# The up-projection's and the last stage's split operands in many memory forms

## The chip, the cores and the metric

The kernel runs on one core of a Trainium2 chip. The metric is the device time in microseconds (us) of one execution, as the median of several runs; lower is better. The engines are named as in the profile: PE is the matrix engine's multiplication, PEld its load of the stationary operand, DVE the vector engine, ACT the scalar engine, POOL the general one, SP the engine that issues most DMAs.

## The reference

One decoder layer on 256 tokens of width 2048: a mixer (mLSTM and RWKV-7 in parallel), cross-attention into 256 memory tokens, and a convolutional gated feed-forward part. All values are float32. The part that the change touches is the last:

```python
def conv_glu_ffn(h, w_up, conv_w, conv_b, w_down):
    u = h @ w_up                                   # (256, 2048) @ (2048, 16384)
    uc = conv_b + sum(conv_w[j] * shift_right(u, CONV_WIDTH - 1 - j) for j in range(CONV_WIDTH))
    gate, up = split_cols(uc, (D_FF, D_FF))
    return (jax.nn.gelu(gate, approximate=True) * up) @ w_down   # (256, 8192) @ (8192, 2048)
...
    h = rms_norm(x, ffn_pre_norm[l])
    x = x + rms_norm(conv_glu_ffn(h, ffn_w_up[l], ffn_conv_w[l], ffn_conv_b[l], ffn_w_down[l]), ffn_post_norm[l])
```

## The kernel before

**Split operands.** PE multiplies in the type float32r, which keeps fewer bits than float32. So each large operand is split in two: `hi` is the value rounded to float32r (ACT writes it) and `lo` is the value minus `hi` (DVE writes it). A product of weights and activations is then three matmuls into the same accumulator: weight `hi` by activation `hi`, weight `hi` by activation `lo`, weight `lo` by activation `hi`. Each matmul first loads a stationary operand of 128 columns (PEld) and then streams a moving operand past it (PE).

**The feed of weights.** All weights come as items of 128 x 1024 float32 (512 KB) by DMA into tiles `raw` (four buffers). `Feed.hi` has ACT cast an item to `wh` (L391), `Feed.lo` has DVE subtract to get `wl` (L421); `wh` and `wl` are tiles of 1152 elements per partition with four buffers each, of which `staged` hands out a view that begins at element 0 or 16. The engines' orders are written out by hand in `run()`: before the matmuls of item i it emits the staging of items up to i + 3, so the staged weights lie some items ahead of PE. The table `KICK` gives 19 items of the earlier stages another view: it begins at element 24 in place of 16, or its second half lies 8 or 24 elements further, so that one or both halves of the item begin 8 elements (32 bytes) off a multiple of 16 elements (64 bytes). Item 18, for instance, has both halves off.

**The up-projection** (tiles `fm`) is 32 blocks of 512 columns. A block is 8 items; an item holds two chunks k of 128 input features. Per chunk and 128 columns the weights are stationary (128 columns of `wh` or `wl`) and the activations `fh`, `fl` (128 x 256 tokens of chunk k) are moving: 2 x 4 x 3 = 24 matmuls an item, 192 a block, 6144 in all. The `hT` tiles `fh` and `fl` hold 16 chunks of 256 elements each and lie apart. After a block DVE and ACT work out the convolution and the gate and leave the result in `ac`. Blocks 0 and 1 are interleaved with each other.

**The last stage** (tiles `tm`) is the down-projection: 2 blocks of 1024 columns, 64 items each, one chunk k per item. Here the activations are stationary: `asplit` splits two chunks of `ac` at a time into a tile `as` (`hi` of both, then `lo` of both), and the weights move, 512 columns at a time: 4 accumulators x 3 = 12 matmuls an item, 1536 in all. The last 4 items of the second block are taken accumulator by accumulator. The norm and the output follow.

`mm` (L181) issues every matmul, `Meter.call` (L66) records most operations of ACT and DVE, so many rows of the profile bear those two lines. The tile `hT` has two buffers; they hold in turn `hh`/`hl`, `mh`/`ml`, `fh`/`fl`, and at the end `gain` and one `z3`.

Of the kernel before, what the change touches and what calls it, by code (L numbers as in the profile page):

```python
# [145 lines left out]
def _layer(ctx, tc, nc, d, dbg):  # L146
# [18 lines left out]
    def hT(name):  # L165
        return mp.tile([P, KD, S], F32R, tag="hT", bufs=2, name=name)
# [12 lines left out]

    def mm(out, lhsT, rhs, start=True, stop=True):  # L180
        pe.matmul(out, lhsT, rhs, start=start, stop=stop, skip_group_check=True)  # L181
# [163 lines left out]
    class Feed:  # L345
        def __init__(self, order):
# [27 lines left out]
        def staged(self, name, r, i):  # L374


            k, c = r.shape[1:]
            kick = KICK.get(i)
# [4 lines left out]
            w = wp.tile([P, 1024 + 128], F32R, tag=name, bufs=4, name=name)  # L383
            return w[:, o:o + k * e].rearrange("p (k c) -> p k c", k=k)[:, :, 0:c]

        def hi(self, upto):
            while self.ns <= min(upto, len(self.src) - 1):
                self.dma(self.ns)
                r = self.raw[self.ns]
                wh = self.staged("wh", r, self.ns)  # L390
                nc.scalar.copy(wh, r)  # L391
                self.st[self.ns] = [wh, None]
                self.ns += 1
# [22 lines left out]
        def lo(self, upto):  # L416
            self.hi(upto)
            while self.nl <= min(upto, len(self.src) - 1):
                r = self.raw.pop(self.nl)
                wl = self.staged("wl", r, self.nl)  # L420
                nc.vector.tensor_sub(wl, r, self.st[self.nl][0])  # L421
                self.st[self.nl][1] = wl
                self.nl += 1
# [10 lines left out]
    def tm_products(o, t, c, wx, first, last):  # L434
        wh, wl, xh, xl = wx
        t = slice(t // P * P, t // P * P + P)
        c = slice(c, c + o.shape[1])
        mm(o, xh[:, t], wh[:, c], start=first, stop=False)
        mm(o, xl[:, t], wh[:, c], start=False, stop=False)
        mm(o, xh[:, t], wl[:, c], start=False, stop=last)  # L440
# [16 lines left out]
    def run():  # L457
        order = visits()
        feed = Feed([("xv" if b is xv else b["kind"], s) for b, c0, c1 in order for s in b["srcs"][c0:c1]])
# [6 lines left out]
        for b, c0, c1 in order:  # L466
# [23 lines left out]
            for ci, s in enumerate(srcs):  # L490
# [13 lines left out]
                for kj in range(s.shape[1]):  # L504
                    xh, xl = b["xs"](k) if kj else ahead
                    first, last = k == 0, k == nk - 1
                    if b["kind"] == "fm":
                        steps = []
                        for m in range(nm):
                            o = banks[m // 2][:, m % 2]  # L510
                            a, c = wh[:, kj, m * P:(m + 1) * P], wl[:, kj, m * P:(m + 1) * P]
                            steps.append([(o, a, xh, first and m % 2 == 0, False), (o, c, xh, False, last),
                                          (o, a, xl, False, False)])
# [14 lines left out]
                    elif b is xv:  # L528
                        for g in range(2):
                            halves(banks, (wh[:, kj], wl[:, kj], xh, xl), first, last, g)  # L530
                    else:
                        for g, o in enumerate(banks):
                            n = o.shape[1]
                            tm_products(o, g * P * n // b["cols"], g * n % b["cols"], (wh[:, kj], wl[:, kj], xh, xl),
                                        first, last)
                            if len(banks) == 4 and g == 1:
                                side.half()
# [59 lines left out]
    hh, hl = hT("hh"), hT("hl")  # L597
# [903 lines left out]
    class Residual:  # L1501
# [8 lines left out]
        def run(self):  # L1510
# [12 lines left out]
            def parts(i, js=(0, 1)):  # L1523
                for j in js:
                    k = i * 2 + j
                    act.activation(hi[:, k], part(xr, i)[:, j], AF.Identity, scale=pcol(gname, k))
                for j in js:
                    k = i * 2 + j
                    dve.scalar_tensor_tensor(lo[:, k], part(xr, i)[:, j], pcol(gname, k), hi[:, k],
# [99 lines left out]
    def mem_prep():  # L1629
        M["mh"], M["ml"] = hT("mh"), hT("ml")  # L1630
# [177 lines left out]
    def start_ffn():  # L1808
# [3 lines left out]
        M["res"] = Residual(st3, "z2", stf, hT("fh"), hT("fl"), "fg", False)  # L1812
# [58 lines left out]
    for b in range(32):  # L1871
        fu = block("fm", W("w_fu", b), fu_xs(b), fu_evac(b),
              before=start_ffn if b == 0 else None, pool_=aux if b == 2 else acc)
        if b < 2:
# [4 lines left out]
    def asplit(k):  # L1879

        if k not in M["as"]:
            n = k // 2
            if k == 126:
                a = C("as", "bg0", [P, 1024], F32R)
            else:
                a = mp.tile([P, 1024 + 128], F32R, tag=f"au{n % 2}", bufs=1, name="as")[:, 0:1024]
            a = a.rearrange("p (i j s) -> p i j s", i=2, j=2)
            a, b_ = a[:, 0], a[:, 1]
            for j in range(2):
                split(a[:, j], b_[:, j], actile((k + j) % 64))  # L1890
# [33 lines left out]
    def load_gain():  # L1924
        M["gain"] = mp.tile([P, D], F32, tag="hT", bufs=2, name="gain")
# [4 lines left out]
    def fd_evac(n):  # L1930

        def gen(ps):
            if n:
                z = mp.tile([P, 2, 1024], F32, tag="hT", bufs=2, name="z3")
# [70 lines left out]
    for n in range(2):  # L2005
        block("tm", W("w_fd", n), ax(n), fd_evac(n), cols=1024, pool_=acc if n else aux,
              tail=4 if n else 0)
# [93 lines left out]
```

## Time and profile before

| | |
|---|---|
| median of 2 runs | 1865.76 us (1865.25 and 1866.28) |
| span of the profiled execution | 1863.2 us; the runs' median lies 2.6 us above it |
| granted PE clock | 0.999 |
| PE busy | 1853.5 us (99%) |
| PEld busy | 1767.5 us (95%) |
| DVE busy | 1295.5 us (70%) |
| ACT busy | 1017.0 us (55%) |
| up-projection, last stage | about 807 to 1507 us, and 1507 to 1856 us of the span |

A row of instructions names the line, the engine, the operation, the tiles as output<-inputs, the shape, and then busy time and the mean of one in ns. PE's matmuls are pipelined: the duration of one (277 ns for 256 columns) is longer than the distance from its start to the next one's start, and that distance is what a stream of them costs. It is read from the chain of waits (time by number of matmuls) or from the starts in the timeline.

### The profile page before, as it was taken

What the parts mean: (1) busy time and instruction counts of PE and PEld (TensorE: products, weight loads), DVE (VectorE), ACT (ScalarE), POOL (GpSimd) and SP (SyncE); (2) the same over time, 40 slices, a digit from 0 to 9 for tenths busy, and PEclk for the clock granted to TensorE, in tenths of its full rate; (3) what the DMA queues carried; (4) which work ended last, traced back from release to release, by engine and by line L of the source; (5) the groups of instructions that cost most, each with busy time, mean ns of one, the idle gap of its engine ahead of it and who ended that gap; (6) DMA issues with size and microseconds to landing.
All of it is one profiled execution on the core that took longest, in us unless ns stands there. A gap on an engine that the chain in (4) does not pass through costs nothing.

```text
span 1863.2 us, 36212 instructions
## 1 busy us (share of the span) xinstructions
PE 1853.5 (99%) x14934; PEld 1767.5 (95%) x14934; DVE 1295.5 (70%) x1832; ACT 1017.0 (55%) x1492; POOL 32.4 (2%) x62
## 2 busy tenths in 40 slices
PE   9999999999999999999999999999999999999998
PEld 9999988999999999999999999999999988888887
DVE  7789777566675857787766667776666775556555
ACT  6876445655454646665554455444445554545544
POOL 0000020000000000000000000000000000000000
PEclk9999999999999999999999999999999999999999
DMA  7556544344555765555666666666666666666664
GB/s 261 186 166 203 180 149 160 136 160 158 172 195 196 277 197 180 165 180 172 202 192 194 196 195 196 185 194 199 195 194 195 197 192 215 194 193 192 194 192 145
DMA packets 98198, 351.47 MB, mean 189 GB/s; under 512 B 11056, under 2 KB 11568, under 8 KB 97648
## 3 DMA queue, kind: packets, MB, share of 16 engines
q1 hardware_dynamic: 97168, 348.01, 58.6%
q8 instruction: 117, 1.92, 0.4%
q10 hardware_dynamic: 864, 1.15, 0.2%
q14 instruction: 49, 0.40, 0.1%
HBM read 347.01 MB, written 2.10 MB: 187 GB/s over the span
## 4 chain that ended last, share of the span: by engine, by line
PE 98%; DVE 1%; DMA 0%; issue 0%; ACT 0%; ACTq 0%; DVEq 0%
PE fm L181 68%; PE tm L181 25%; PE gram L181 0%; DVE wl L421 0%; PE Y L181 0%; DMA w<-in_w_in_dram 0%; PE num L181 0%; PE lv L181 0%; DVE ql L66 0%; PE X L181 0%; PE U L181 0%; PE zg L181 0%; DVE z L66 0%; PE zwa L181 0%; PE xsc L181 0%
## 5 line engine op out<-in xcount | busy, mean ns | idle before, releaser
L421 DVE TENSOR_TENSOR wl<-raw,wh 128x1024 fp32r<-128x1024 f32 (+1 forms) x639 | 774.8, 1218 | 412.7 <-ACT wh L391 406.5
L391 ACT CAST wh<-raw 128x1024 fp32r<-128x1024 f32 (+1 forms) x639 | 663.6, 1043 | 476.0 <-PE fm L181 362.5
L181 PE MATMUL fm<-fh,wh 128*128 128x256 f32 x2048 | 564.2, 277 | 0.6 <-DVE fh L66 0.6
L181 PE MATMUL fm<-fh,wl 128*128 128x256 f32 x2048 | 563.2, 276 | 0.0
L181 PE MATMUL fm<-fl,wh 128*128 128x256 f32 x2048 | 563.2, 276 | 0.0
L181 PEld LDWEIGHTS fm<-fh,wh 128*128 128x128 f32 x2048 | 383.6, 188 | 0.8 <-DVE fh L66 0.8
L181 PEld LDWEIGHTS fm<-fl,wh 128*128 128x128 f32 x2048 | 383.5, 188 | 0.0
L181 PEld LDWEIGHTS fm<-fh,wl 128*128 128x128 f32 x2048 | 383.5, 188 | 0.0
L181 PE MATMUL tm<-wh,as 128*128 128x512 f32 x1024 | 315.1, 389 | 0.0
L181 PE MATMUL fm<-hh,wh 128*128 128x256 f32 x1024 | 284.3, 280 | 1.7 <-ACT wh L402 1.5
L181 PE MATMUL fm<-hl,wh 128*128 128x256 f32 x1024 | 281.7, 277 | 0.0
L181 PE MATMUL fm<-hh,wl 128*128 128x256 f32 x1024 | 281.5, 277 | 0.1
L181 PEld LDWEIGHTS tm<-wh,as 128*128 128x128 f32 x1024 | 192.2, 188 | 39.8
L181 PE MATMUL tm<-wl,as 128*128 128x512 f32 x512 | 199.2, 389 | 0.0
L181 PEld LDWEIGHTS fm<-hh,wh 128*128 128x128 f32 x1024 | 191.9, 188 | 3.4 <-ACT wh L402 1.7
L181 PEld LDWEIGHTS fm<-hl,wh 128*128 128x128 f32 x1024 | 191.9, 188 | 0.1
L181 PEld LDWEIGHTS fm<-hh,wl 128*128 128x128 f32 x1024 | 191.5, 188 | 0.3 <-DVE wl L421 0.3
L181 PEld LDWEIGHTS tm<-wl,as 128*128 128x128 f32 x512 | 96.1, 188 | 19.9
L66 ACT CAST as<-ac 128x256 fp32r<-128x256 f32 x128 | 45.6, 404 | 110.8 <-PE tm L181 110.8
L66 DVE TENSOR_TENSOR as<-ac,as 128x256 fp32r<-128x256 f32 x128 | 48.6, 421 | 61.7 <-ACT as L66 61.7
L181 PE MATMUL fm<-mgh,wh 128*128 128x256 f32 x256 | 70.9, 277 | 0.0
L181 PE MATMUL fm<-mgl,wh 128*128 128x256 f32 x256 | 70.8, 276 | 0.0
(406 smaller groups left out, 2225.0 us busy)
## 6 DMA issues: line engine op xcount, KB each, us to landing
raw<-in_w_fu_dram SPq DMA_DIRECT2D x256, 512.0 KB, 4.1
raw<-in_w_in_dram SPq DMA_DIRECT2D x152, 512.0 KB, 3.6
raw<-in_w_fd_dram SPq DMA_DIRECT2D x128, 512.0 KB, 3.9
raw<-in_w_br_dram SPq DMA_DIRECT2D x32, 512.0 KB, 4.1
raw<-in_w_mo_dram SPq DMA_DIRECT2D x32, 512.0 KB, 4.3
raw<-in_w_xk_dram SPq DMA_DIRECT2D x8, 512.0 KB, 4.2
raw<-in_w_xv_dram SPq DMA_DIRECT2D x8, 512.0 KB, 3.6
raw<-in_w_xq_dram SPq DMA_DIRECT2D x8, 512.0 KB, 4.0
```

The costliest lines, as they stand in the source:

```text
L66: return f(out, *a, **k)
L181: pe.matmul(out, lhsT, rhs, start=start, stop=stop, skip_group_check=True)
L391: nc.scalar.copy(wh, r)
L421: nc.vector.tensor_sub(wl, r, self.st[self.nl][0])
```

## The change

The `hi` and `lo` of one operand now share one tile, and where in it they lie follows tables. All numbers in the tables are elements of 4 bytes. `halves_of(v, g)` cuts a view in two: with g = 0 the first and the second half, with g = 1 the even and the odd elements, with a larger g alternating groups of g elements.

- `STATIONARY`, one entry per up-projection block from block 2 on: the weights' form. (0, a, b) is `hi` beginning at element a and `lo` at element 1152 + b of a `w2` tile of 2304. (1, a) is `hi` and `lo` element by element in turn from element a on. Blocks 2, 12, 13, 30 and 31 have both at multiples of 16; blocks 3 to 11 have both off a multiple of 16; blocks 14, 16, 19, 21 have only `lo` off and 15, 17, 18, 20 only `hi`; blocks 22 to 29 are element by element.
- `MOVING`, one entry per pair of chunks of the up-projection (so one per item of each block): the activations' form, (g, offset). Items 0 and 1 of a block are two halves at offsets 0 and 16, item 2 at offset 8, items 3, 4, 5, 6, 7 alternate in groups of 1, 4, 8, 32 and 2.
- `STREAMED`, per pair of items of the last stage, eight entries in rotation: the moving weights at offsets 0, 16, 8, 24, then alternating in groups of 16 and of 4, then two entries with plain halves but another width: 512 columns are taken as 256 + 256, or as 384 + 128. The last four items of the second block keep the plain form and 512.
- `HELD`, per 16 chunks of the last stage over both blocks: the stationary activations at offsets 0, 16, 8, 24, then element by element, then offset 4, element by element from 16, and 0.

What is computed is the same, and the output accumulators have the same shapes. The tile `hT` becomes one tile of 16 x 528 elements with one buffer; the earlier users of it get two halves of it that lie as before.

```diff
-    def hT(name):
-        return mp.tile([P, KD, S], F32R, tag="hT", bufs=2, name=name)
+    def hT(name, dt=F32R):
+        return mp.tile([P, KD * 528], dt, tag="hT", bufs=1, name=name)
+    MOVING = [(0, 0), (0, 16), (0, 8), (1, 0), (4, 0), (8, 0), (32, 0), (2, 0)]
+    STATIONARY = [(0, 16, 16), (0, 16, 16), (0, 0, 0), (0, 2, 2), (0, 4, 4), (0, 6, 6), (0, 8, 8), (0, 12, 12),
+                  (0, 20, 20), (0, 24, 24), (0, 28, 28), (0, 30, 30), (0, 16, 0), (0, 0, 16), (0, 16, 24), (0, 24, 16),
+                  (0, 16, 8), (0, 8, 16), (0, 20, 16), (0, 16, 20), (0, 12, 16), (0, 16, 12), (1, 0), (1, 4), (1, 8),
+                  (1, 12), (1, 16), (1, 20), (1, 24), (1, 28), (0, 16, 16), (0, 16, 16)]
+    STREAMED = [(0, 0, 512), (0, 16, 512), (0, 8, 512), (0, 24, 512), (16, 0, 512), (4, 0, 512), (0, 0, 256), (0, 0, 384)]
+    HELD = [(0, 0), (0, 16), (0, 8), (0, 24), (1, 0), (0, 4), (1, 16), (0, 0)]
+    class Halves:
+        def __init__(self, v, i):
+            v = v.rearrange("p (k c) -> p k c", k=KD)
+            self.v = [halves_of(v[:, k, o:o + 512], g)[i] for k in range(KD) for g, o in (MOVING[k // 2],)]
...
+    def halves_of(v, g):
+        n = v.shape[1] // 2
+        if g == 0:
+            return v[:, 0:n], v[:, n:2 * n]
+        if g == 1:
+            v = v.rearrange("p (l i) -> p i l", i=2)
+        else:
+            v = v.rearrange("p (l i g) -> p i l g", i=2, g=g)
+        return v[:, 0], v[:, 1]
...
+            lo = name == "wl"
+            if not lo:
+                self.pairs[i] = wp.tile([P, 2304], F32R, tag="w2", bufs=4, name="w2")
+            w = self.pairs[i]
+            form = self.form.get(i)
+            if form:
+                g, o = form[0], form[1]
+                if g:
+                    return halves_of(w[:, o:o + 2048], g)[lo].rearrange(
+                        "p (k l) -> p k l" if g == 1 else "p (k l) g -> p k l g", k=k)
+                o = 1152 + form[2] if lo else o
+                return w[:, o:o + 1024].rearrange("p (k c) -> p k c", k=k)
...
-    def tm_products(o, t, c, wx, first, last):
+    def tm_products(o, t, c, wx, first, last, width=512):
...
+        for a in range(0, n, width):
+            b = min(a + width, n)
+            q, hi, lo = o[:, a:b], part_of(wh, c + a, c + b), part_of(wl, c + a, c + b)
+            mm(q, xh, hi, start=first and a == 0, stop=False)
+            mm(q, xl, hi, start=False, stop=False)
+            mm(q, xh, lo, start=False, stop=last)
...
+            if b.get("ups", 0) > 1:
+                form[at] = STATIONARY[b["ups"]]
+            if "down" in b and (b["down"], j) < (1, 60):
+                g, o, n = STREAMED[j // 2 % 8]
+                form[at] = (g, o, o)
...
+            g, o = HELD[k // 16]
...
-                a = mp.tile([P, 1024 + 128], F32R, tag=f"au{n % 2}", bufs=1, name="as")[:, 0:1024]
-            a = a.rearrange("p (i j s) -> p i j s", i=2, j=2)
-            a, b_ = a[:, 0], a[:, 1]
+                a = mp.tile([P, 1024 + 128], F32R, tag=f"au{n % 2}", bufs=1, name="as")[:, o:o + 1024]
+            a, b_ = [v.rearrange("p (j s) g -> p j s g" if g > 1 else "p (j s) -> p j s", j=2) for v in halves_of(a, g)]
```

Two places of the engines' orders show what moves. The first is PE's order in the last stage, at chunk 14 of the first block, ahead and now (`tm_n` are the four accumulators, `as` the stationary activations, the last numbers the output's shape). Before:

```order
L181 MATMUL tm_18531<-wh_18782,as_18800 128x512 x2
L181 MATMUL tm_18531<-wl_18784,as_18800 128x512
L181 MATMUL tm_18532<-wh_18782,as_18800 128x512 x2
L181 MATMUL tm_18532<-wl_18784,as_18800 128x512
L181 MATMUL tm_18533<-wh_18782,as_18800 128x512 x2
L181 MATMUL tm_18533<-wl_18784,as_18800 128x512
L181 MATMUL tm_18534<-wh_18782,as_18800 128x512 x2
L181 MATMUL tm_18534<-wl_18784,as_18800 128x512
```

And now:

```order
L230 MATMUL tm_18005<-w2_18245,as_18262 128x384 x3
L230 MATMUL tm_18005<-w2_18245,as_18262 128x128 x3
L230 MATMUL tm_18006<-w2_18245,as_18262 128x384 x3
L230 MATMUL tm_18006<-w2_18245,as_18262 128x128 x3
L230 MATMUL tm_18007<-w2_18245,as_18262 128x384 x3
L230 MATMUL tm_18007<-w2_18245,as_18262 128x128 x3
L230 MATMUL tm_18008<-w2_18245,as_18262 128x384 x3
L230 MATMUL tm_18008<-w2_18245,as_18262 128x128 x3
```

Twelve matmuls of 512 columns have become twelve of 384 and twelve of 128, each with its own load of a stationary operand. Where the width is 256, there are 24 of 256 in their place. Over both blocks 28 items are so cut, 14 with 256 and 14 with 384, and PE has 336 matmuls more.

The second is DVE's order in the up-projection, with the semaphores that a row waits for (`us`, `tg`, `tu`, `ac` belong to the convolution and the gate of the block before). Before:

```order
L66 SCALAR_TENSOR_TENSOR tu_15599<-us_15595,cv_9869,tu_15599 128x254 [waits DVE_49]
L421 TENSOR_TENSOR wl_15678<-raw_15566,wh_15676 128x1024 [waits DMAHW7_49,PE_49,Activation_49]
L66 TENSOR_TENSOR ac_15694<-tg_15596,tu_15598 128x256
L66 TENSOR_TENSOR ac_15694<-tg_15597,tu_15599 128x256 [waits DVE_49]
L421 TENSOR_TENSOR wl_15711<-raw_15605,wh_15709 128x1024 [waits DMAHW0_49,PE_49,Activation_49]
```

And now:

```order
L66 SCALAR_TENSOR_TENSOR tu_15161<-us_15157,cv_9601,tu_15161 128x254 [waits DVE_49]
L484 TENSOR_TENSOR w2_15236<-raw_15128,w2_15236 128x1024 [waits DMAHW7_49,Activation_49]
L66 TENSOR_TENSOR ac_15253<-tg_15158,tu_15160 128x256
L66 TENSOR_TENSOR ac_15253<-tg_15159,tu_15161 128x256 [waits DVE_49]
L484 TENSOR_TENSOR w2_15268<-raw_15166,w2_15268 128x1024 [waits DMAHW0_49,Activation_49]
```

The order of the operations on DVE and on ACT is the same. DVE's subtraction no longer waits for PE, since the buffer is now taken when ACT writes `hi`; ACT's cast waits for the last reader of both halves.

More of the change, by code (lines that the diff above doesn't have):

```diff
@@ L345, in _layer, with __init__ @@
     class Feed:
-        def __init__(self, order):
+        def __init__(self, order, form):
+            self.form, self.pairs = form, {}
             self.kind = [k for k, s in order]
```

66 lines of the change are left out of this document (46 added, 20 removed).

## The prediction

> **What bounds the kernel now.** I read the clock and the span first, then the engines' shares and the chain of waits, then the chain in order of time, then the stretches of the two stages that change.
>
> ```profile
> core 0: 1863.2 us, clock 0.999
> PE 1853.5 (99%) x14934; PEld 1767.5 (95%) x14934; DVE 1295.5 (70%) x1832; ACT 1017.0 (55%) x1492; POOL 32.4 (2%) x62
> PE 98%; DVE 1%; DMA 0%; issue 0%; ACT 0%; ACTq 0%; DVEq 0%
> 938.94 568.50 PE fm L181 x5016
> 1507.44 348.20 PE tm L181 x1536
> 939.00:1507.00 568.00, 392.87 (x526) 1.00 0.64 194
> ```
>
> The clock is full, and the chain is PE for 98%. In the two stages it is nothing else: 568.50 / 5016 = 113.3 ns from one matmul of 256 columns to the next, 348.20 / 1536 = 226.7 ns for 512, which is exactly twice as much. So the price goes by the streamed column (0.443 ns), and no fixed price per matmul or per load shows. The last row is DVE alone in the up-projection: 392.87 of 568 us, 69%. PE has no idle time to give or to hide in: whatever makes a matmul start later lengthens the kernel one for one.
>
> How near is the load of the stationary operand to becoming the limit? The four loads ahead of matmuls with one moving column show it, since there nothing else takes time:
>
> ```profile
> 755.16 0.52 PEld L181 LDWEIGHTS st<-ones,stx 128*128 128x128 f32 x4 [0.26 <-DVE stx L66]
> L181 PEld LDWEIGHTS fm<-fh,wh 128*128 128x128 f32 x2048 | 383.6, 188 | 0.8 <-DVE fh L66 0.8
> ```
>
> Four loads of 188 ns each fill 520 ns, so they start (520 - 188) / 3 = 111 ns apart. With 113.3 ns per matmul the up-projection has only 2 ns to spare; with 226.7 the last stage has 115. That bounds any gain: if a form took moving columns faster, the loads would hold the 6144 matmuls at 111 ns, 14 us less, 0.8%.
>
> **The change part by part.** First the narrower width. Of 28 cut items 14 go as 256 + 256, 2 x 113.3 = 226.7 ns, nothing lost. The other 14 x 12 = 168 matmuls become 384 (170.0 ns at 0.443 a column) and 128. By the column 128 would cost 56.7 and the whole nothing; but each has a load, and those keep 111 ns. 170.0 + 111 - 226.7 = 54 ns, times 168: **+9 us**, between 0 and 9. I take 9, since three of 128 follow each other and leave a load nothing to hide behind.
>
> Second, stationary weights off the 64-byte grid. The items of KICK in the kernel before show that. These starts are of item 18, both halves 32 bytes off, and of a later one:
>
> ```profile
> 50.93 0.28 PE L181 MATMUL fm<-hh,wh 128*128 128x256 f32 x1
> ...
> 53.09 0.28 PE L181 MATMUL fm<-hh,wh 128*128 128x256 f32 x1
> 717.96 0.28 PE L181 MATMUL fm<-mh,wh 128*128 128x256 f32 x1
> ...
> 719.13 0.28 PE L181 MATMUL fm<-ml,wh 128*128 128x256 f32 x1
> ```
>
> Between the first two lie 18 steps, 120 ns each; between the others 10, 117 ns each. So off the grid costs 4 to 7 ns a matmul, with no other change. Blocks 3 to 11 are off for all 9 x 192 = 1728 matmuls; of the eight blocks with one half off, `hi` is stationary twice and `lo` once in three, so half of 1536 are off: 768. Third, the 8 x 192 = 1536 loads element by element: no row shows one. Their ends are 0 (the load keeps its 111 ns) and twice a load, 222 ns, that is +109 each. I take 4.7, as for the off-grid loads, the nearest row with a load from an unusual place. Together 2496 + 1536 = 4032 matmuls at 4.7 ns; one in eight runs under item 3, below, where the moving side hides it: 3528 x 4.7 = **+17 us**, between 0 (if the other offsets and the steps are free) and 25 at 7 ns; with doubled loads 1344 x 109 = 146 more.
>
> Fourth, the moving activations. All moving operands of the trace are contiguous and on the grid, so the price has to be argued from how much slack the stream has. Two rows speak:
>
> ```profile
> 859.13 0.44 PE xt L1920 x4
> L1920 PE MATMUL xt<-con,xr x32: 270/273/273, 859.0 to 938.7; 128*128 128x128 f32 x32
> ```
>
> The transposes stream 128 columns of 4 bytes in 0.44 / 4 = 110 ns, 0.86 ns a column. That is half the rate, and a little less than twice 0.443 = 0.886: the fast stream pays some 3% that the slow one does not, as a stream would that is just short of data. If so, a read that fetches two neighbours and throws one away halves the rate: item 3 (element by element) has 32 x 24 = 768 matmuls, and each would take 226.7 in place of 113.3, **+87 us**. Its ends are 0 and 87, and I take 87. The groups of 2 (item 7) use whole pairs; if the unit fetched is 16 bytes, they halve too, +87 more. I leave them at the small price and keep the 87 for the range. Items 2, 4, 5 and 7 in the seven blocks with loads on the grid: 7 x 4 x 24 = 672 matmuls at between 0 and 7 ns, 3.5 taken: **+2 us**. Item 6 (groups of 32, runs of 128 bytes) costs 0.
>
> By the Trainium skill's page "TensorE: Matmul & The Clock Gate", section "Part 1: The HAM clock gate", a warm stream takes 1 / 2.4 GHz = 0.417 ns a column and 2.5 ns a matmul, 109 ns here by an estimate; the trace's 113.3 is above that, and its surcharge goes by the column.
>
> Fifth, the last stage. Loads have 115 ns to spare, so off-grid or stepped stationary activations (80 of the 128 chunks) hide behind the moving weights up to a doubled load. The moving weights are off the grid in a quarter of the items and grouped by 16 or 4 in another: 768 matmuls at 0 to 14 ns (7 per 256 columns), 4 taken: **+3 us**.
>
> Sixth, DVE and ACT. They write `hi` and `lo` with a step of two elements in blocks 22 to 29 and read `hi` so. Rows on what steps cost DVE:
>
> ```profile
> L421 DVE TENSOR_TENSOR wl<-raw,wh 128x1024 fp32r<-128x1024 f32 x631 | 768.7, 1223 | 409.7 <-ACT wh L391 403.5 <-PE fm L181 4.7
> L66 DVE TENSOR_TENSOR ac<-tg,tu 128x256 f32<-128x256 f32 x64 | 24.1, 419 | 0.0
> L66 DVE TENSOR_TENSOR mt<-cmt,con 128x256 f32<-128x256 f32 x8 | 4.6, 619 | 0.0
> L391 ACT CAST wh<-raw 128x1024 fp32r<-128x1024 f32 x631 | 658.1, 1048 | 470.4 <-PE fm L181 360.5 <-PE tm L181 89.9 <-ACT wh L391 4.8
> 939.00:1507.00 568.00, 255.80 (x209) 1.00 0.64 194
> ```
>
> `cmt` is read with a step of 32 elements: 200 ns more for 256, 0.78 ns an element. The last row is `wl` alone: 255.8 of DVE's 392.9 us, so the rest is 137 us in 568, 5.3 in a block's 21.8. With eight subtractions of 1.22 that is 15.0 us, and PE's 21.8 covers it. One stepped operand makes 2.0 us of each (21.4 in all, still covered), two make 2.8 (27.9: not covered). But item 3 then takes 24 x 113 ns = 2.7 us longer too, so PE's block is 24.5 or more. Taken: 0; at worst 27.9 - 24.5 = 3.4 a block, 27 us in eight. ACT's cast is 1048 ns; doubled it is 16.8 us a block beside about 4 of its own, covered.
>
> The queues: no instruction is moved past another on ACT, DVE, POOL or SP. ACT's cast now waits for the last reader of `lo` as well, one matmul (113 ns) later than for `hi`; its idle time in the row above, mostly for PE, is 470 us, and DVE's subtraction, which follows it, has three items' lead. Cost 0; if the lead were gone, 256 items x 0.1 us, 26 us.
>
> The sum: 1863.2 + 9 + 17 + 87 + 2 + 3 = 1981 us of span, and 2.6 us more for the median of the runs, which lies that far above the span: **1984 us**, +6%.
>
> **The rivals.** *Steps are free for the moving side, places cost a little.* Without the 87 us, but with item 3's 768 matmuls now at up to 7 ns and its loads not hidden, +3: 1984 - 87 + 3 = **1900 us**, +1.8%. For it: 0.443 ns is the same for 256 and for 512 columns, so it may be the stream's own pace and no shortage of data. Against it: the 0.86 of the half-rate stream.
> A rule of the Trainium skill gives this case: "SBUF — State Buffer", section "Door 1: The DMA port swizzle", says that memory lines are 16 bytes and that two hits per line give full bandwidth. Every second float32 is two hits a line, so by it the sum is 1900. The page "Vector Engine (DVE) Microarchitecture Reference", section "5.2 Measured stream behaviour on trn2", says that a port keeps its rate only for runs of at least two adjacent words, measured on DVE; by that, item 3 slows and item 7 does not. The trace has no stepped PE read and cannot part them.
>
> *Nothing but the cut width costs anything* (not slower). The off-grid price of KICK's items could belong to their stages, where each item stands alone between others; a whole block in one form could settle into the 113.3 step, since the load's 111 still fits. Then only the 384 + 128 remains: 1863.2 + 9 + 2.6 = **1875 us**, +0.5%. It decides at the point where loads start no more than 113 ns apart. Against it: item 18 holds 120 ns over 18 steps without settling.
>
> *A wider unit is fetched.* That 32 bytes off the grid matter at all speaks for a unit of 64 bytes. Then groups of 1, 2, 4 and 8 all use half of each unit: 4 x 768 matmuls at +113.3, 348 us, plus 9 + 17 + 3: **2243 us**, and with stepped loads at 222 ns in the other four items (768 x 109 = 84 us) 2327. Against it: an off-grid load would then fetch nine units in place of eight, 111 x 9 / 8 = 125 ns, and the rows say 117 and 120.
>
> *The pairs halve too* (unit of 16 bytes): 1984 + 87 - 2 = **2069 us**. This is the forecast's own upper end.
>
> That the forms are not there as told is excluded by the order: PE's rows have the widths of 384, 128 and 256.
>
> **How the numbers follow.** About 2% (37 us, from 1829 to 1903) is what a measurement of this kernel can tell from no change. The forecast, single elements starving the moving stream with the pairs open, has 0.45, its own range 1970 to 2085. Free steps with small prices: 0.27, at 1885 to 1920. Only the width: 0.14, at 1866 to 1885. The wider unit: 0.12. Faster through some better form: 0.02, and by the bound of 14 us hardly by 2%. A range from 1874 to 2085 leaves out the wider unit, the gain and about half of a tenth at the low end, under 0.2. Slower by over 2%: 0.45 + 0.12 + a little over half of 0.27 = 0.72; within 2%: 0.27; faster: 0.01.
>
> **What would show it.** In the timeline of any block: item 3's steps at 227 ns (forecast), 113 to 120 (free steps); item 7's at 113 to 120, or 227 if the unit is 16 bytes; items 4 and 5 at 227 with a wider unit. Blocks 3 to 11 at 117 to 120 and blocks 2, 12, 13, 30 and 31 at 113 in items 0, 1 and 6. Blocks 22 to 29 at 222 in items 0 and 1 if loads double. In the last stage items of 384 + 128 take 3.4 us, not 2.7. The DVE rows of `w2` above 2.8 us, with PE idle on DVE in blocks 22 to 29, would show that the cover failed. The forecast is wrong if item 3 keeps 120 ns or less.

## The result and the profile after

The changed kernel takes **2087.94 us** (median of 2 runs, 2087.56 and 2088.33) against 1865.76: the ratio is 1.119, with a 95% interval from 1.116 to 1.123. It is slower, by more than the forecast of 1984 us, and lies 3 us above the range's upper end of 2085.

The page of the changed kernel, first the clock and span, then the engines' busy time and the shares of the chain:

```profile
core 0: 2085.7 us, clock 0.999
PE 2075.5 (100%) x15270; PEld 1966.1 (94%) x15270; DVE 1298.7 (62%) x1832; ACT 1026.5 (49%) x1492; POOL 32.4 (2%) x62
PE 97%; DVE 1%; issue 0%; DMA 0%; ACT 0%; ACTq 0%; DVEq 0%
```

The chain in order of time, its two long pieces (start, us, engine, output tile, line, count), and the up-projection's stretch for DVE alone (a row of a stretch gives from:to in us, its length, the engine's busy time and in brackets how many of its instructions touch it; the last three numbers are the granted PE clock, the busy share of the DMA engines and what they moved in GB/s):

```profile
972.71 737.72 PE fm L230 x5016
1710.43 367.83 PE tm L230 x1872
```

```profile
972.70:1710.40 737.70, 395.79 (x526) 1.00 0.49 150
```

The clock is full as before and the chain is PE throughout, so no engine or wait has taken PE's place. The same 5016 matmuls of the up-projection take 737.7 us in place of 568.5. From the first start of `fm` to its end the stage has grown by 203.4 us, and the last stage by 19.6 (348.2 to 367.8): together the span's 222.5 within half a microsecond. DVE's work over that stretch is 395.8 us, 392.9 before. All of the loss is in PE's own matmuls.

Where in a block does it lie? These are the stretches of the eight items of block 20; each is touched by the 24 matmuls of the item and two or three at its borders. First the kernel before, item 0 (all eight read 2.72):

```profile
1246.06:1248.78 2.72, 2.72 (x27) 1.00 0.66 208
```

Then the changed one, items 0 to 7:

```profile
1371.17:1374.05 2.88, 2.88 (x26) 1.00 0.00 0
1374.05:1376.90 2.85, 2.85 (x27) 1.00 0.63 184
1376.90:1379.74 2.84, 2.84 (x27) 1.00 0.36 88
1379.74:1385.24 5.50, 5.50 (x27) 1.00 0.63 203
1385.24:1388.08 2.84, 2.84 (x26) 1.00 0.21 79
1388.08:1390.90 2.82, 2.82 (x27) 1.00 0.63 186
1390.90:1393.78 2.88, 2.88 (x27) 1.00 0.63 182
1393.78:1399.27 5.49, 5.49 (x27) 1.00 0.65 191
```

An item took 2.72 us before, 113.3 ns a matmul. Item 3 (element by element) now takes 5.50, 229 ns a matmul, and so does item 7 (groups of 2) with 5.49. The other six take 2.82 to 2.88 us, 118 to 120 ns. It is so in every block: over blocks 2 to 31 item 3 grew by 83.2 us, item 7 by 83.0, the other six by 24.9 together; with their share of blocks 0 and 1 items 3 and 7 cost 88.5 us each and everything else in the up-projection about 26. The six light items lie at 116 to 123 ns in all kinds of blocks: also in blocks 12, 13, 30 and 31, whose weights are on the 64-byte grid, and in blocks 22 to 29, whose weights are loaded element by element.

In the last stage, the stretches of chunks 8, 13, 14 and 29 of the first block, 2.72 us each before. Chunk 8 streams groups of 16, chunk 14 is cut into 384 + 128, and chunks 13 and 29 are cut into 256 + 256, with the stationary activations 0 and 64 bytes into their tile:

```profile
1732.45:1735.34 2.89, 2.89 (x14) 1.00 0.66 203
1746.69:1749.57 2.88, 2.88 (x26) 1.00 0.57 171
1749.56:1752.96 3.40, 3.40 (x27) 1.00 0.58 176
1792.79:1795.51 2.72, 2.72 (x27) 1.00 0.55 131
```

And the two staging operations in a stretch of 56 us within blocks 22 to 29, whose weights are written element by element:

```profile
L484 DVE TENSOR_TENSOR w<-raw,w 128x1024 fp32r<-128x1024 f32 x16 | 19.6, 1225 | 22.7 <-ACT w L454 22.7
L454 ACT CAST w<-raw 128x1024 fp32r<-128x1024 f32 x16 | 18.4, 1147 | 31.4 <-PE fm L230 31.4
```

In block 20 the subtraction takes 1224 ns and the cast 1046: the step of two elements costs DVE nothing and ACT 101 ns a cast, with PE still without idle time.

### The profile page after: what moved, and what is told of

It reads as the page before. It is cut to its first block, busy times and chain, and to the rows that moved or that the text cites. A ratio compares the mean times of both kernels' runs of the same rounds, so it can differ in the third digit from the quotient of the medians.

```text
span 2085.7 us, 36843 instructions
## 1 busy us (share of the span) xinstructions
PE 2075.5 (100%) x15270; PEld 1966.1 (94%) x15270; DVE 1298.7 (62%) x1832; ACT 1026.5 (49%) x1492; POOL 32.4 (2%) x62
## 4 chain that ended last, share of the span: by engine, by line
PE 97%; DVE 1%; issue 0%; DMA 0%; ACT 0%; ACTq 0%; DVEq 0%
PE fm L230 70%; PE tm L230 23%; DVE w L484 0%; PE gram L230 0%; PE Y L230 0%; DMA w<-in_w_in_dram 0%; PE num L230 0%; DVE ql L66 0%; PE lv L230 0%; PE X L230 0%; PE U L230 0%; DVE stx L66 0%; PE zg L230 0%; PE zwa L230 0%; DVE z L66 0%
## 5 line engine op out<-in xcount | busy, mean ns | idle before, releaser
L484 DVE TENSOR_TENSOR w<-raw,w 128x1024 fp32r<-128x1024 f32 (+1 forms) x639 | 775.0, 1217 | 586.5 <-ACT w L454 585.2
L454 ACT CAST w<-raw 128x1024 fp32r<-128x1024 f32 (+1 forms) x639 | 669.8, 1053 | 697.8 <-PE fm L230 556.9
L230 PE MATMUL fm<-fp,w 128*128 128x256 f32 x6144 | 902.7, 314 | 0.6 <-DVE fp L66 0.6
L230 PEld LDWEIGHTS fm<-fp,w 128*128 128x128 f32 x6144 | 869.5, 195 | 32.0 <-DVE fp L66 0.8
L230 PE MATMUL tm<-w,as 128*128 128x512 f32 (+2 forms) x1872 | 368.0, 359 | 0.0
L230 PEld LDWEIGHTS tm<-w,as 128*128 128x128 f32 x1872 | 315.7, 190 | 52.1 <-DVE w L484 0.3
L230 PE MATMUL fm<-hp,w 128*128 128x256 f32 x3072 | 358.9, 278 | 2.1 <-ACT w L465 1.8
L230 PEld LDWEIGHTS fm<-hp,w 128*128 128x128 f32 x3072 | 353.2, 188 | 4.0 <-ACT w L465 2.0
L230 PE MATMUL tm<-w,hp 128*128 128x512 f32 (+1 forms) x480 | 104.0, 373 | 0.4 <-DVE qk L66 0.4
L230 PE MATMUL fm<-mgh,w 128*128 128x256 f32 x512 | 88.0, 277 | 0.0
```

Source lines behind the costliest of these rows:

```text
L454: nc.scalar.copy(wh, as_form(r, wh))
L484: nc.vector.tensor_sub(wl, as_form(r, wl), self.st[self.nl][0])
```

## The experiments

All kernels are the changed one with edits in its tables, in the size of a chunk's slot (the elements that the tile of the activations keeps for one chunk) or in the weights' places; each computes the same thing. "Plain" is an operand in two contiguous halves. Lines taken out in a diff are those of the kernel that it starts from: the change itself, or the layout alone with all tables plain, with the slot that the text names. Of most runs the long pieces of the chain are given, the up-projection's (`fm`) and the last stage's (`tm`); divided by their counts they are ns per matmul of 256 columns, and of 512. Two runs of the layout alone lay 0.8 us apart and eight runs of the slot of 512 elements 1.5 us; the other kernels of this section ran once, at a granted clock of 0.999 or 1.000.

### Which table costs what

**The new layout alone**: all four tables plain, so that only the shared tiles and the slot of 528 elements per chunk are left of the change.

```diff
-    MOVING = [(0, 0), (0, 16), (0, 8), (1, 0), (4, 0), (8, 0), (32, 0), (2, 0)]
-    STATIONARY = [...]
-    STREAMED = [...]
-    HELD = [...]
+    MOVING = [(0, 0)] * 8
+    STATIONARY = [(0, 16, 16)] * 32
+    STREAMED = [(0, 0, 512)] * 8
+    HELD = [(0, 0)] * 8
```

> All four tables plain: every operand contiguous and on the 64-byte grid, all widths 512, only the shared tiles of the change stay. Layout theory (the shared tiles themselves make plain items take 118 ns): the up-projection keeps about 118 ns a matmul, 6144 x 5 = 31 us over before, some 1897 us. Forms theory (only the tables matter): 113.3 and 226.7 ns as before, 1866 us.

```profile
941.69 590.08 PE fm L227 x5016
1531.76 348.41 PE tm L227 x1536
```

1889.92 us beside 1863.78 of the kernel before (ratio 1.014, 1.011 to 1.017). The last stage is as before, but the up-projection is 117.6 ns a matmul with no odd form left in it. The layout itself costs 26 us, which the prediction had nowhere.

**The moving forms alone**: `MOVING` as in the change, the other three plain.

```diff
-    MOVING = [(0, 0)] * 8
+    MOVING = [(0, 0), (0, 16), (0, 8), (1, 0), (4, 0), (8, 0), (32, 0), (2, 0)]
```

> Only MOVING as in the change; weights and the last stage plain. Both theories: items 3 and 7 at 227 to 229 ns, 1536 x 114 = 175 us. Disturbance theory (a stepped item throws loads and stream into a slower pace that plain items do not leave by themselves): items 0, 1 and 6 stay at 117 to 119 although all is on the grid, 1866 + 175 + 4608 x 5 = 2064 us. Place theory (an item is slow only through its own off-grid operands): items 0, 1 and 6 at 113.3, item 2 perhaps slower, 2041 to 2050 us.

```profile
972.00 731.92 PE fm L227 x5016
```

2061.61 us. The items' means are 117.1, 116.6, 117.5, **228.6**, 118.4, 118.4, 120.1, **227.5** ns. The two long items need nothing of the weights' forms. Groups of 4, 8 and 32 (118.4, 118.4 and 120.1) lie at most 3.5 ns above the contiguous items beside them.

**The change without items 3 and 7**: these two entries plain, all else as changed.

```diff
-    MOVING = [(0, 0), (0, 16), (0, 8), (1, 0), (4, 0), (8, 0), (32, 0), (2, 0)]
+    MOVING = [(0, 0), (0, 16), (0, 8), (0, 0), (4, 0), (8, 0), (32, 0), (0, 0)]
```

> The change with items 3 and 7 contiguous, all else as it is. Both theories: 2088 - 177 = 1911 us if the other items keep 118 ns. Disturbance theory, with the stepped items as the disturber: blocks 2, 12, 13, 30 and 31 fall to 113.3 in items 0, 1, 3, 6 and 7, about 1905 us, and off-grid blocks stay at 117 to 120. If groups of 4 and 8 or off-grid items disturb as well, those blocks stay near 118 and the time is 1911 us or a few us more.

```profile
943.38 596.17 PE fm L230 x5016
```

1916.66 us: two table entries hold 171 of the 222 us. The last stage is unchanged to the hundredth (367.83).

**The stationary weights' forms alone**:

```diff
-    STATIONARY = [(0, 16, 16)] * 32
+    STATIONARY = [(0, 16, 16), (0, 16, 16), (0, 0, 0), (0, 2, 2), ..., (1, 28), (0, 16, 16), (0, 16, 16)]
```

> Only STATIONARY as in the change. Place theory: blocks 3 to 11 at 117 to 120 ns, blocks 14 to 21 near 116, blocks 22 to 29 at 118 to 121, blocks 2, 12, 13, 30, 31 at 113.3: 1866 + 20 = about 1886 us. Disturbance theory: the blocks on the grid are slow too where they follow an off-grid one: 1866 + 5760 x 5 ns = 1895 us. Wide-unit theory for loads (stepped loads twice as long): blocks 22 to 29 at 220 ns, 1866 + 1536 x 107 ns = 2030 us.

```profile
942.21 595.22 PE fm L230 x5016
```

1895.18 us, only 5 more than the layout alone. All blocks lie between 116 and 121 ns a matmul, those with loads element by element at 118 to 121. A stepped load does not take twice the time.

The parts add up: the moving forms with the layout +197.8 us, the stationary forms beyond the layout +5.3, the last stage +19.6 make 222.7; measured were 222.2.

### What a stepped stream is charged by

Items 3 and 7 double and groups of 4 do not, which fits a stream that fetches whole units of 16 bytes (places are counted from the start of a tile). But so would a rule that charges any run shorter than four elements, wherever it begins. The next kernel tells these apart, with groups that begin 8 bytes off: groups of 4 then touch twice as many 16-byte lines, groups of 8 one and a half times as many. The slot is 544 elements here (2176 bytes, 17 x 128), and the weights' tile is 2240 with `lo` at 1120.

```diff
-        return mp.tile([P, KD * 528], dt, tag="hT", bufs=1, name=name)
+        return mp.tile([P, KD * 544], dt, tag="hT", bufs=1, name=name)
-    MOVING = [(0, 0)] * 8
+    MOVING = [(0, 0), (0, 2), (8, 0), (8, 2), (4, 0), (4, 2), (32, 2), (0, 0)]
-                self.pairs[i] = wp.tile([P, 2304], F32R, tag="w2", bufs=4, name="w2")
+                self.pairs[i] = wp.tile([P, 2240], F32R, tag="w2", bufs=4, name="w2")
```

> 544 elements per chunk (a multiple of 128 bytes), weights and last stage plain. Items of a block: 0 and 7 plain, 1 contiguous but 8 bytes off, 2 and 4 in groups of 8 and 4 on the grid, 3, 5 and 6 in groups of 8, 4 and 32 that begin 8 bytes off a 16-byte line. Theory of the 16-byte line (a matmul lasts as long as its distinct 16-byte lines at 113.3 / 64 = 1.77 ns each): item 1 touches 65 lines, 115 ns; item 3 96 lines, 170 ns; item 5 128 lines, 227 ns; item 6 72 lines, 127 ns; items 2 and 4 64 lines, 113 to 120 ns. Pair theory (whole pairs of elements are enough) or a theory of large strides (the step itself costs): items 3, 5 and 6 as 2 and 4, 113 to 120 ns. In us: 1864 + 768 x (57 + 113 + 14) ns = 2005 and up to 20 more by the first, 1864 to 1890 by the second.

2041.98 us, 17 above what the expectation allowed for the 16-byte line at most. The items of block 20, from item 2 to item 6, and the last stage:

```profile
1356.37:1359.23 2.86, 2.86 (x26) 1.00 0.15 57
1359.23:1363.29 4.06, 4.06 (x27) 1.00 0.62 222
1363.29:1366.13 2.84, 2.84 (x25) 1.00 0.61 185
1366.13:1371.59 5.46, 5.46 (x27) 1.00 0.61 186
1371.59:1374.82 3.23, 3.23 (x25) 1.00 0.03 10
```

```profile
1674.18 358.42 PE tm L227 x1536
```

| form of the moving operand | 16-byte lines touched | ns by 113.3 / 64 = 1.77 a line | measured |
|---|---|---|---|
| groups of 8 on the line, item 2 | 64 | 113.3 | 119.2 |
| groups of 4 on the line, item 4 | 64 | 113.3 | 118.2 |
| contiguous, 8 bytes off, item 1 | 65 | 115 | 120.4 |
| groups of 32, 8 bytes off, item 6 | 72 | 127 | 134.5 |
| groups of 8, 8 bytes off, item 3 | 96 | 170 | 169.2 |
| groups of 4, 8 bytes off, item 5 | 128 | 227 | 227.6 |

The same group of 4 takes 118 or 228 ns, only by where it begins: both consist of whole pairs, so the pair is not the unit; and run and step are the same, so the pattern is not it either. The count of 16-byte lines gives the two large prices within 1 ns. The light items pay 5 to 6 ns more than their count, and item 6, at 134.5 for 127, pays 7; its first step behind item 5 alone takes 156. These small prices, some 24 us, and a last stage of 358.4 in place of 348.4 us are most of what the time lies above the 2005 us of that count. The tables of the last stage are plain; it differs only by `lo` of the weights at 1120 elements, which is 128 bytes beyond a multiple of 256.

### What the small price comes from

**A slot of 512 in place of 528 elements**, tables plain:

```diff
-        return mp.tile([P, KD * 528], dt, tag="hT", bufs=1, name=name)
+        return mp.tile([P, KD * 512], dt, tag="hT", bufs=1, name=name)
```

> All tables plain, as in the first run, but the shared tile of the activations has 512 elements per chunk in place of 528, so that the moving operands of all chunks begin at the same place modulo 128 bytes (0), 64 bytes from the weights' (64). Relation theory (the two read streams of PE go at 113.3 ns only where moving and stationary addresses stay a fixed distance apart modulo 128 bytes; 528 elements are 16.5 times 128 bytes, so even and odd chunks alternate): 113.3 ns again, 1864 us. If the sharing of one tile by hi and lo weights is the cause instead: 117.6 ns as in the first run, 1890 us.

```profile
937.62 568.50 PE fm L227 x5016
```

1864.76 us beside 1863.64 (ratio 1.0005, 0.9994 to 1.0016): the up-projection is at 568.50 to the hundredth of the kernel before. With 528 elements (2112 bytes, 16.5 x 128) a chunk's place modulo 128 bytes changes from one chunk to the next; with 512 it is always the same. The shared tiles as such cost nothing. Stretches of 12 matmuls show it, the two chunks of item 2 in block 20 and the first of item 3; first with 528:

```profile
1266.29:1267.68 1.39, 1.39 (x14) 1.00 0.07 29
1267.68:1269.10 1.42, 1.42 (x14) 1.00 0.75 141
1269.10:1270.52 1.42, 1.42 (x14) 1.00 0.56 228
```

With 512, item 2:

```profile
1250.33:1251.69 1.36, 1.36 (x14) 1.00 0.16 63
1251.69:1253.05 1.36, 1.36 (x14) 1.00 0.54 81
```

The third stretch says more: that chunk begins on a multiple of 128 bytes, but not of 256, and is slow too. Over blocks 7 to 30 of the layout alone the last six steps of a chunk take 113.4 ns where it begins on a multiple of 256 bytes, and 119.1, 117.9 and 119.0 where it begins 64, 128 or 192 beyond. So the moving operand's place seems to count modulo 256.

The next runs were made for another idea, that the distance between where the stationary and the moving operand lie matters, modulo 128 bytes: in the kernel before and with the slot of 512, weights begin 64 bytes after a multiple of 128 and activations on one. **Weights at element 0 from block 2 on**, so at distance 0, slot 512:

```diff
-    STATIONARY = [(0, 16, 16)] * 32
+    STATIONARY = [(0, 16, 16)] * 2 + [(0, 0, 0)] * 30
```

> As the run with 512 elements per chunk, all plain, but the weights begin 0 and not 64 modulo 128 bytes from block 2 on, the same as the activations: everything is on the 64-byte grid and regular. Relation theory with the distance of 64 as the good one for 256 columns: 117 to 120 ns, 1864 + 5760 x 5 = 1893 us. Theory that any constant distance on the grid will do: 113.3 ns, 1864 us.

```profile
943.38 601.91 PE fm L227 x5016
```

1903.07 us (1893 expected), and a steady 601.91 / 5016 = 120.0 ns. The weights are on the 64-byte grid here, so it is not the grid that decides.

**All the stationary forms with the slot of 512** puts a row of places side by side:

```diff
-    STATIONARY = [(0, 16, 16)] * 32
+    STATIONARY = [(0, 16, 16), (0, 16, 16), (0, 0, 0), (0, 2, 2), ..., (1, 28), (0, 16, 16), (0, 16, 16)]
```

> Only STATIONARY as in the change, 512 elements per chunk, so that each block holds its weights at one fixed distance from the activations modulo 128 bytes. Relation theory: each block settles at its own steady step: 113.3 at a distance of 64 (blocks 30, 31), 120.0 at 0 (block 2), the others between; blocks 22 to 29 (stepped loads) at 113 to 121. Off-grid theory: blocks 3 to 11 at 117 to 120 whatever the distance, and block 2 on the grid too is 120 only by its distance. Either way 1885 to 1905 us. Wide-unit theory for loads: blocks 22 to 29 at 220 ns, which the run of the weights' forms alone already speaks against.

1894.21 us. Blocks 7, 12, 25 and 30 (192 matmuls each):

```profile
966.50:990.16 23.66, 23.66 (x194) 1.00 0.55 180
1081.72:1104.33 22.61, 22.61 (x194) 1.00 0.62 187
1377.76:1401.08 23.32, 23.32 (x194) 1.00 0.59 181
1493.12:1514.88 21.76, 21.76 (x194) 1.00 0.60 193
```

Each block has its own steady price: 8 bytes off (block 3) 115.5 ns in the items that nothing else disturbs, 48 bytes (block 7) 123.2, on the grid but with `lo` at 0 (block 12) 117.8, element by element from 0 (block 22) 120.0, from 12 (block 25) 121.5, and 64 bytes (block 30) 113.3. Nothing is cheaper than the place that the kernel before had. A matmul with a stepped load takes at most 8 ns more than that.

**Both sides shifted alike**: slot 528 again, and the second chunk of a weight item also 528 elements after the first, so that the distance stays at 64 modulo 128.

```diff
+                if self.kind[i] == "fm":
+                    return w[:, o:o + 2 * 528].rearrange("p (k c) -> p k c", k=k)[:, :, 0:c]
```

> All tables plain, 528 elements per chunk as in the change, but the second chunk of each weight item begins 16 elements further, so that weights and activations alternate together and stay 64 bytes apart modulo 128. Relation theory: 113.3 ns in all blocks from 2 on, about 1865 us. Theory of the fixed place (the moving operand has to begin at 0 modulo 128): odd chunks stay slow, some 117 to 118 ns, 1885 to 1890 us.

```profile
942.20 586.62 PE fm L227 x5016
```

1886.54 us, 117.0 ns: a miss. The first chunk of items 0, 2, 4 and 6 settles after some three matmuls (121, 116, 114, 114, 113, 113); all other chunks stay at about 118, the first chunk of items 1, 3, 5 and 7 too. The distance alone is not the rule. The chunks that settle are again those whose activations begin on a multiple of 256 bytes.

**The period**, slot 512: weights at 16, 48, 80 and 112 elements, which are 64 bytes modulo 128 in different places modulo 512; and the stationary activations of the last stage at 0, 32, 64 and 96 elements.

```diff
-    STATIONARY = [(0, 16, 16)] * 32
-    HELD = [(0, 0)] * 8
+    STATIONARY = [(0, 16, 16)] * 4 + [(0, 16, 16)] * 7 + [(0, 48, 48)] * 7 + [(0, 80, 80)] * 7 + [(0, 112, 112)] * 7
+    HELD = [(0, 0), (0, 32), (0, 32), (0, 64), (0, 64), (0, 96), (0, 96), (0, 0)]
```

> 512 elements per chunk, all plain; the weights of up-projection blocks 4 to 10 begin at element 16, of 11 to 17 at 48, of 18 to 24 at 80, of 25 to 31 at 112: the distance to the activations is 64, 192, 320 and 448 bytes, always 64 modulo 128. In the last stage the held activations begin at 0, 32, 64 and 96 elements, always 0 modulo 128 bytes. Theory of a period of 128 bytes: 113.3 ns in all blocks and 226.7 ns in the whole last stage, 1864 us. Theory of a longer period (256 or 512): the blocks at 192 and 448, or all but the first group, at 117 to 120, and the last stage at 233 where the held offset is 32 and 96 (or also 64): 1870 to 1890 us.

```profile
938.83 568.50 PE fm L227 x5016
1507.33 352.83 PE tm L227 x1536
```

1869.44 us. The up-projection is at 113.3 in all blocks, so the weights' place, the stationary side's, counts modulo 128 bytes there. In the last stage a chunk takes 226.7 ns per 512 columns with the stationary side at 0 or 256 bytes and 232.4 at 128 or 384: there the period is 256. The longer last stage of the groups 8 bytes off fits that: its `lo`, moving, lay 128 bytes beyond a multiple of 256. **The last stage at 64 bytes**, slot 512:

```diff
-    HELD = [(0, 0)] * 8
+    HELD = [(0, 16)] * 8
```

> 512 elements per chunk, all plain, but the stationary activations of the last stage begin 64 bytes further, so that their distance to the moving weights is 64 and not 0 modulo 128 bytes. Relation theory with 0 as the good distance for 512 columns (the change's own run had 235 where the held offset was 16 and the streamed 0): 233 to 240 ns, 1864 + 1500 x 6 to 13 ns = 1873 to 1884 us. If 64 is the good distance for every width: 226.7 or less, 1864 us or below.

```profile
1506.91 358.47 PE tm L227 x1536
```

1874.66 us, a steady 233.3 ns: with 512 columns 64 bytes is a bad place and 0 the good one, the other way round than with 256 columns. It is the width that turns it round and not the stage: the changed kernel's chunks 13 and 29 above are of the same stage at 256 columns, and take 240.0 ns per 512 columns (120.0 a matmul) with the stationary side at 0, 226.7 (113.3) at 64.

**The whole change with a slot of 544**, which keeps a chunk's place modulo 128 bytes, but not modulo 256:

```diff
-        return mp.tile([P, KD * 528], dt, tag="hT", bufs=1, name=name)
+        return mp.tile([P, KD * 544], dt, tag="hT", bufs=1, name=name)
```

The weights' tile is 2240 with `lo` at 1120, as for the groups 8 bytes off.

> The whole change, but 544 in place of 528 elements per chunk, so even and odd chunks lie the same. Relation theory: items 0 and 6 fall to 113 to 116 in the blocks with weights at a distance of 64 (13 for hi, 12 for lo, 30, 31), item 1 (64 bytes further) is at 120 there, the off-grid blocks stay at 117 to 120: 2075 to 2085 us. If 528 were the whole of the small price: 2088 - 24 = 2064 us.

```profile
976.23 738.45 PE fm L230 x5016
```

2092.29 us, no better than the change, where 2064 to 2085 was expected; the last stage is at 368.35. This does not show that a steady slot is worth nothing beside other forms, since 544 elements do not give the pace back even to plain items. The kernel with groups 8 bytes off has the same slot, and there the two chunks of item 7, which is plain and followed by a plain item, take:

```profile
1374.95:1376.33 1.38, 1.38 (x15) 1.00 0.71 125
1376.33:1377.75 1.42, 1.42 (x14) 1.00 0.61 248
```

The first begins on a multiple of 256 bytes and settles at 113.3 ns; the second begins 128 beyond and stays at 118.9. Both kernels also moved `lo` of the weights, and no run parts the two edits.

The multiple of 256 is read off the steps of runs made for other questions; no run was made to test it. It has exceptions: in the change without items 3 and 7, the first chunk of item 3 in blocks 30 and 31 begins 128 beyond and settles all the same; and in the change itself the first chunk of block 30, on a multiple of 256, stays at 118 ns.

**Steps without the rest**: slot 512, all plain but items 3 and 7.

```diff
-    MOVING = [(0, 0)] * 8
+    MOVING = [(0, 0), (0, 0), (0, 0), (1, 0), (0, 0), (0, 0), (0, 0), (2, 0)]
```

> 512 elements per chunk, all plain except items 3 (element by element) and 7 (groups of 2) of each up-projection block. Both: items 3 and 7 at 227 to 229 ns. If a stepped item leaves no trace behind it: the other six items at 113.3 ns, 1864 + 1536 x 115 = 2041 us. Disturbance theory (a stepped item shifts the two streams and the following plain items stay at 117 to 118): 2041 + 4608 x 4.5 = 2062 us.

2047.05 us. Block 20 from item 3 to item 5, and below it the first four and the second four matmuls of item 4:

```profile
1368.59:1374.07 5.48, 5.48 (x26) 1.00 0.70 210
1374.07:1376.85 2.78, 2.78 (x27) 1.00 0.25 99
1376.85:1379.57 2.72, 2.72 (x27) 1.00 0.59 185
```

```profile
1374.07:1374.58 0.51, 0.51 (x7) 1.00 0.70 289
1374.58:1375.03 0.45, 0.45 (x7) 1.00 0.39 155
```

The doubled price stands by itself, 228.6 ns in both items. Behind a stepped item the steps are 152, 122, 118, 114 and then 113: about 52 ns are paid once, and the stream is back at its pace. Here plain items beside stepped ones do settle, on a slot that is a multiple of 256 bytes.

No version beat both kernels: the best, the plain one with the slot of 512, equals the kernel before.

## Why the prediction was wrong

The sum of what was measured closes: 1863.2 + 177 for items 3 and 7 + 26 for the rest of the up-projection + 19.6 for the last stage = 2085.8 us of span, 2085.7 in the profile. Against the prediction's terms:

- **Item 3, +87: right in size**, and only in part in mechanism. It was taken at 226.7 ns and measured 228 to 234; +88.5 us. That the stream fetches elements that it throws away fits, but in units of four and not of two. The row that carried the argument is weak: the four transposes of 128 columns in 0.44 us are 110 ns apart, which is also the 111 ns at which the prediction has loads start, and in the changed kernel float32r matmuls of 128 columns come 111 ns apart too. So that row need not show a half-rate stream at all, and the right size was in part luck.
- **Item 7, left at the small price: this is the step that failed.** It was stated as "the groups of 2 (item 7) use whole pairs", with 87 us kept for the range only. The pace is set by 16-byte lines, and a group of 2 uses half of each: 227.5 ns with the moving forms alone, +88.5 us in the change. The prediction chose the pair because a half-rate stream at 0.86 ns a column was read as a stream just short of data. That row could not say how wide the unit is, and the sum should have weighed the two widths as equals. The rival "the pairs halve too" was the true case, at 2069 us; it missed by some 19 us, most of them from the small prices.
  The Trainium skill's page "SBUF — State Buffer", section "Door 1: The DMA port swizzle", has two hits per 16-byte line as enough for full bandwidth. This case does not agree for PE's moving operand: items 3 and 7 make two hits per line and take 228.6 and 227.5 ns in place of 113.3. The Trainium skill's page "Vector Engine (DVE) Microarchitecture Reference", section "5.2 Measured stream behaviour on trn2", has runs of two adjacent words at full rate on DVE. That does not carry over to PE, whose groups of 2 are those of item 7. The 16-byte line itself fits the runs, and it is the whole line that counts.
- **The grid and the stepped loads, +17, and +2 for the items in on-grid blocks: too small and for the wrong reason.** They measured 26. The prediction read the 117 and 120 ns of the early stages as the price of being off a 64-byte grid, and so charged the blocks with weights on the grid next to nothing; it expected 113 in their items 0, 1 and 6, which take 117 to 120. The layout alone, with everything on the grid, costs 26 us (117.6 ns), and a place on the grid can cost 120.0 steadily. What was overlooked is the slot of 528 elements, which moves a chunk's place every time: with 512 in its place the 26 us are gone. The forms then add only 5 us to it; with the slot of 512 they cost 27 by themselves. The two do not add.
- **Stepped loads not doubled: right.** 118 to 123 ns in blocks 22 to 29; the bound of 146 us was not needed.
- **384 + 128, +9: right.** An item takes 3.40 us as foretold. In chunk 14 the steps of one accumulator are 60, 111 and 112 ns for the three of 128 columns, and the first of 384 behind them takes 233 in place of 175: the loads keep 111 ns, as the four loads with one moving column had said. By the items' means of 282 to 296 ns per 512 columns it is 10 us.
- **The last stage's places, +3: too small.** About 9.6 us. Where the held and the streamed offset agree modulo 128 bytes, the two items of a pair take 227.5 to 228.5 ns on average, and held 16 with streamed 32 bytes takes 226.7 as well; elsewhere it is mostly 230 to 236, and with groups of 16 elements 237 to 242. Of the 9.6 us, 1.6 are in the items of 256 + 256, which the prediction had at nothing lost: 227 to 228 ns per 512 columns with the held side 64 bytes in, 234 to 240 elsewhere, as the two stretches above show.
- **DVE and ACT, 0: right.** In blocks 22 to 29 the subtraction takes 1225 ns, elsewhere 1224; the cast 1147 in place of 1046, hidden. In them DVE is busy 15.1 us of a block's 28.1.
- **Queues and waits, 0: right.** The chain shows none.

The upper end of the range, 16 us above the 2069 of that rival, was meant for just this case; it fell 3 us short for the layout and the last stage.

## What to carry to other kernels

Keep the moving operand of float32r matmuls in runs of whole, aligned 16-byte lines: interleaving two operands in groups of 1 or 2, or in larger groups that begin inside a line, costs up to a factor of two on PE, while DVE took a step of two elements free and the stationary side at no more than 8 ns a matmul. Keep the places of both operands in one fixed relation through a long run of matmuls: here a slot of 528 elements cost 1.4% with not one strided access, and one of 512 (2048 bytes) nothing. A multiple of 128 bytes is not enough for the slot (544 elements); a multiple of 256 is what the steps suggest. When a trace can't tell which unit a fetch has, price the case by each unit and give them like chances; a cost kept "for the range" is a term left out of the sum.

## What the hardware showed that was not expected

- A stream of float32r matmuls takes 113.3 ns per 256 contiguous columns, and about 1.77 ns per 16-byte line of the moving operand that it touches, where lines are more than the columns need: 169.2 ns for 96 lines (170 by the count), 227.6 for 128 (227).
- The price also goes by where the operands lie in their tiles: 113.3 or 120.0 ns a matmul of 256 columns with the weights 64 or 0 bytes from a multiple of 128 (up to 123 in between), and 226.7 or 233.3 for 512 columns with the stationary operand at 0 or 64. With the weights at 64, a chunk of contiguous activations settled at 113.3 on a multiple of 256 bytes and stayed at 117 to 121 elsewhere, with few exceptions. After a change some matmuls pass before it settles (about 52 ns behind a stepped item).
- Open: why 64 is the good place for 256 columns and 0 for 512, and why the stationary side's period is 128 bytes for the one and 256 for the other; whether the moving side's 256 holds in a run made for it; where the tiles themselves begin, which no trace tells; why groups of 32 that begin 8 bytes off take 134.5 ns and not 127; why groups of 4 and 8 on the line take 118 and 119 and not 113.3. That it is a conflict of the load's and the stream's reads would fit that both sides' places matter, but no run here shows it.
